# Loading x first, sharing its squares and the weight remainders with GpSimd, and handing PSUM banks over singly, in the first stage of a decoder block

## The chip, the cores and the metric

The kernel runs on one core of a Trainium2 chip. A core has TensorE (matrix products into PSUM; the profile calls its products PE and its weight loads PEld), VectorE (DVE), ScalarE (ACT), GpSimd (POOL) and SyncE (SP), which here only issues transfers (DMA). Each engine works through its own queue of instructions in the order in which they were written into it; between engines, semaphores make an instruction wait. SBUF is the core's working memory of 128 partitions; PSUM holds eight banks of 128 x 512 float32 numbers. The metric is the time of one execution in microseconds (us); lower is better.

## The reference

One block of a decoder with 512 tokens and 2048 channels. What the first stage computes, and what reads it:

```python
c_act = jax.nn.silu(c)
mod = c_act @ w_ada[l] + b_ada[l]                       # 2048 x 12288
sh1, sc1, gt1, sh2, sc2, gt2 = jnp.split(mod[:, None, :], N_MOD, axis=-1)
h = _rmsnorm(x, norm1_g[l]) * (1.0 + sc1) + sh1         # x * rsqrt(mean(x*x) + eps) * g
p = h @ w_in[l]                                         # 2048 x 4384
y_rwkv = _rwkv7_mixer(p[..., :N_RWKV_COLS], ...)
y_pool = _pool_mixer(p[..., N_RWKV_COLS:], ...)
mix = jnp.concatenate([y_rwkv, y_pool], axis=-1) @ w_out[l]
x = x + gt1 * mix
h = _rmsnorm(x, norm2_g[l]) * (1.0 + sc2) + sh2
x = x + gt2 * _conv_ffn(h, w_up[l], conv_w[l], conv_b[l], w_down[l])
...
return _rmsnorm(x, norm_f_g)
```

The RWKV mixer runs eight pairs of heads (0 to 7), each from columns r, k and v of p and from three low-rank tiles that all pairs share; the pooling mixer has four groups of 256 channels.

## The kernel before, in words

Activations lie transposed, channels on partitions, as 16 tiles of 128 x 512. Weights are float32, and a product keeps their precision by a split: `split_weights` (L101) loads a 128 x 512 tile of weights (`wraw`, four buffers), ScalarE casts it to a shorter type (`whi`, L105, three buffers), and VectorE subtracts that from the original (`wlo`, L107, three buffers). Activations are split the same way into `ah` and `al`. `mm3` (L110) then makes three products into one PSUM tile: whi with ah, whi with al, wlo with ah.

The first stage (L168 to L256) goes like this. SP issues the constant tables (`vec`, `cmat` with the identity and the ones, `masks`, `mlev`, `lanei`, `prec`), then c, broadcast to all partitions (`cb`). ScalarE applies silu to cb; a row of it is stored to DRAM (`cact`) for later stages. x arrives in eight transfers of two tiles. For the norm, ScalarE squares each tile of x and VectorE adds it to one sum (`sacc`); four small products with ones (`pst`) sum over the partitions, ScalarE takes the square root, VectorE the reciprocal and spreads it on a diagonal (`rdiag`), one more product (`psb`) broadcasts it, and ScalarE copies it to SBUF (`rs`).

The loop over the 16 tiles k follows, and is called a turn below. Per k, two tiles of w_ada (`wa`, 1 MiB each, four buffers) are each multiplied by cb and summed along the row by one VectorE instruction (`jk`, L202), which gives one column of scale (`part` 1) and of shift (`part` 0). Small VectorE instructions finish them (`gsc`, L204; `mod`, L206). `modulate` (L135) makes `h` on VectorE (L137), `ah` on ScalarE (L138) and `al` on VectorE (L139). Two tiles of weights of the input projection are split, and 24 products go into eight PSUM tiles `pf0` to `pf7`, which fill all eight banks and stay open over the 16 turns.

Behind the loop the eight banks are read out: `shift` (L222) mixes each token with the one before it, on ScalarE and then VectorE, for the three low-rank tiles (`xwa`, `xg1`, `xg2`, which then go through tanh and sigmoid on ScalarE) and for r, k and v of pair 0; the last two banks are copied into `upad` for pooling group 3. The pool of banks `ps0` is then closed, and the pool `psa` (tiles `mm`, `pa`, `pb` and others) takes the same eight banks. In the middle stage, `win_pair` (L591) projects r, k and v of a further pair as three window tiles of 16 x 3 products each, `pool_group` (L258) does a pooling group, `stage_a`, `stage_b` and `stage_c` do a pair of heads, and `ada_rest` (L327) goes on with w_ada in small pieces (`jkr`).

The order on each engine is found when the program is built: a scheduler with its own costs takes instructions by priority, which is the order of the Python code unless `hp()` (L611) raises a block. A tile that reuses memory waits for what used it: by default the first tile in a reused pool waits for everything in the pool that lay there before. With `reuse_waits="tile"`, which the later stages' pools already have, a tile waits only for those earlier tiles whose memory it takes.

Of the kernel before, what the change touches and what calls it, by code (L numbers as in the profile page):

```python
# [53 lines left out]
def block_kernel(ctx, tc, a, out, stop=None, dbg=None):  # L54
# [7 lines left out]
    vec = cp.tile([P, NCOL], F32, tag="vec", name="vec")  # L62
    nc.sync.dma_start(vec, a["vec"][:, :])
    cmat = cp.tile([P, 5, P], F32, tag="cmat", name="cmat")
    nc.sync.dma_start(cmat, a["cmat"][:, :, :])
    ident, bones, bmean, cent, ones = (cmat[:, i, :] for i in range(5))
    masks = cp.tile([P, 4, P], F32, tag="masks", name="masks")
    nc.sync.dma_start(masks, a["mask4"][:, :, :])
    mlev = cp.tile([P, 2, 64], F32, tag="mlev", name="mlev")
    nc.sync.dma_start(mlev, a["mlev"][:, :, :])  # L70
    scanm = cp.tile([P, NC, 129], F32, tag="scanm", name="scanm")
    nc.gpsimd.memset(scanm, 1.0)
    nc.gpsimd.memset(scanm[:, :, 0:1], 0.0)
    lanei = cp.tile([64, 16, 16], F32, tag="lanei", name="lanei")
    nc.sync.dma_start(lanei, a["lanei"][:, :, :])
    prec = cp.tile([P, 16], F32, tag="prec", name="prec")
    nc.sync.dma_start(prec, a["prec"][:, :])

    def col(name, i):
        return vec[:, COLS[name] + i : COLS[name] + i + 1]  # L80
# [17 lines left out]
    b1p = cp.tile([P, KT], F32, tag="b1p", name="b1p")  # L98
    V.tensor_scalar_add(b1p, cols("b_ada", 16, 32), 1.0)

    def split_weights(src):  # L101
        raw = wp.tile([P, WC], F32, tag="wraw", name="wraw", bufs=4)
        nc.sync.dma_start(raw, src)
        hi = wp.tile([P, WC], F32R, tag="whi", name="whi", bufs=3)
        S.copy(hi, raw)  # L105
        lo = wp.tile([P, WC], F32R, tag="wlo", name="wlo", bufs=3)
        V.tensor_tensor(lo, raw, hi[:, :].bitcast(F32), op=ALU.subtract)  # L107
        return hi, lo

    def mm3(ps, wh, wl, xh, xl, start, stop):  # L110
# [54 lines left out]
    p0ctx = ExitStack()  # L165
    p0 = p0ctx.enter_context(tc.tile_pool(name="p0", bufs=1))
    if True:
        cb = p0.tile([P, D], F32, tag="cb", name="cb")  # L168
        nc.sync.dma_start(cb, a["c"][0:1, :].partition_broadcast(P))
        S.activation(cb, cb, AF.Silu)  # L170
        nc.sync.dma_start(cact, cb[0:1, :])
        xs = []
        for i in range(8):
            xt = p0.tile([P, 2, T], F32, tag=f"x{i}", name=f"x{i}")
            nc.sync.dma_start(xt, a["xT"][:, 2 * i : 2 * i + 2, :])
            xs += [xt[:, 0, :], xt[:, 1, :]]
        rstd = p0.tile([P, T], F32, tag="rs0", name="rs0")
        with tc.tile_pool(name="ps00", bufs=1, space=PSUM) as ps00:
            pst = ps00.tile([P, NC], F32, tag="st", name="pst")
            acc = p0.tile([P, T], F32, tag="sacc", name="sacc")  # L180
            for k in range(KT):
                if k == 0:
                    S.activation(acc, xs[k], AF.Square)
                    continue
                sq = p0.tile([P, T], F32, tag="sq", name="sq", bufs=2)
                S.activation(sq, xs[k], AF.Square)
                V.tensor_add(acc, acc, sq)
            rms_stats(pst, acc)
            psb = ps00.tile([P, T], F32, tag="bc", name="psb")
            rms_bcast(psb, rms_rows(p0, pst, NC), NC)  # L190
            S.copy(rstd, psb)
        ps0ctx = ExitStack()
        ps0 = ps0ctx.enter_context(tc.tile_pool(name="ps0", bufs=1, space=PSUM))
        pf = [ps0.tile([P, T], F32, tag=f"pf{i}", name=f"pf{i}") for i in range(8)]
        H = []
        for k in range(KT):
            for part in (1, 0):
                j = part * 16 + k
                wa = p0.tile([P, D], F32, tag="wa", name="wa", bufs=4)
                nc.sync.dma_start(wa, a["ada1"][j, :, :])  # L200
                jk = p0.tile([P, D], BF16, tag="jk", name="jk", bufs=1)
                V.scalar_tensor_tensor(jk, wa, 1.0, cb, op0=ALU.mult, op1=ALU.mult,  # L202
                                       accum_out=mod[:, j : j + 1])
            V.scalar_tensor_tensor(gsc1[:, k : k + 1], mod[:, 16 + k : 17 + k], b1p[:, k : k + 1],  # L204
                                   col("n1", k), op0=ALU.add, op1=ALU.mult)
            V.tensor_add(mod[:, k : k + 1], mod[:, k : k + 1], col("b_ada", k))  # L206
            h = p0.tile([P, T], F32, tag="h", name="h", bufs=2)
            hi, lo = slots(k)
            modulate(hi[:, :], lo[:, :], h, xs[k], rstd, gsc1[:, k : k + 1], mod[:, k : k + 1])
            H.append((hi, lo))  # L210
            for i0 in range(0, 8, WC // P):
                wh, wl = split_weights(a["win0"][k, :, i0 * P : i0 * P + WC])
                for ii in range(WC // P):
                    sl = slice(ii * P, (ii + 1) * P)
                    mm3(pf[i0 + ii], wh[:, sl], wl[:, sl], *H[k], start=k == 0, stop=k == KT - 1)
        p0ctx.close()


        actx = ExitStack()
        ra = actx.enter_context(tc.tile_pool(name="ra", bufs=1))  # L220
        if True:
            def shift(ps, m, dst):  # L222
                S.activation(dst, ps, AF.Copy, scale=drv[:, m : m + 1])
                V.scalar_tensor_tensor(dst[:, 1:T], ps[:, 0 : T - 1], col("mu", m), dst[:, 1:T],
                                       op0=ALU.mult, op1=ALU.add)

            def ring(name):
                return ring16(name)[:, 16:]

            def ring16(name):  # L230
                return ra.tile([P, 16 + T], F32, tag="ring", name=name, bufs=7)

            xwa = ra.tile([P, T], F32, tag="xwa", name="xwa")
            shift(pf[0], 24, xwa)
            S.activation(xwa[0:64, :], xwa[0:64, :], AF.Tanh)
            xg1 = ra.tile([P, T], F32, tag="xg1", name="xg1")
            shift(pf[1], 25, xg1)
            S.activation(xg1, xg1, AF.Sigmoid)
            xg2 = ra.tile([P, T], F32, tag="xg2", name="xg2")
            shift(pf[2], 26, xg2)  # L240
            S.activation(xg2, xg2, AF.Sigmoid)

            def vtile(name):
                return ra.tile([P, T], F32, tag="v", name=name, bufs=2)

            rkv0 = []
            for i, m in ((3, 0), (4, 8), (5, 16)):
                t = vtile("v") if i == 5 else ring("rkv")
                shift(pf[i], m, t)
                rkv0.append(t)  # L250

            upad = [ring16("upad") for i in range(2)]
            for i in range(2):
                V.memset(upad[i][:, 0:16], 0.0)
                S.copy(upad[i][:, 16:], pf[6 + i])  # L255
            ps0ctx.close()  # L256

    def pool_group(gi):  # L258
        win = WINS[gi]
# [30 lines left out]
                last_mix.append(split_act(14 + d, mx))  # L290

    psctx = ExitStack()
    psa = psctx.enter_context(tc.tile_pool(name="psa", bufs=1, space=PSUM))

    def mmtile():
        return psa.tile([P, T], F32, tag="mm", name="mm", bufs=2)
# [314 lines left out]
    def hp():  # L611
        return tc.high_priority(offset=100000)

    pool_group(3)
    with hp():
        q = start_pair(0)
        stage_b(0, q)
    win_pair(1)
    for p in range(NP):
        if p + 1 < NP:  # L620
            if p + 2 < NP:
# [320 lines left out]
```

## Time and profile before

| | |
|---|---|
| median of 3 runs | 2465.12 us (2463.72 to 2469.42) |
| the profiled execution | 2465.06 us, of it 2463.3 us between the first and the last instruction (the span) |
| TensorE products | 2355.7 us busy, 96% of the span |
| VectorE | 1450.8 us, 59% |
| ScalarE | 912.6 us, 37% |
| GpSimd | 2.7 us, 13 instructions, all of them fills |
| DMA | 367.40 MB, 149 GB/s on average |

A row of the order in time has the start, the duration, the engine, the line of the code, the operation, output and inputs by the program's names, shapes, how many were merged into the row, and in brackets how long the engine had been idle and what ended that. In a table of stretches, each engine's busy time stands with its count of instructions in brackets, then TensorE's granted clock, the share of time the 16 DMA engines were busy, and GB/s. A group of instructions has its line, engine and operation, the count, busy time and mean duration in nanoseconds, and the idle time ahead of it.

### The profile page before, as it was taken

What the parts mean: (1) busy time and instruction counts of PE and PEld (TensorE: products, weight loads), DVE (VectorE), ACT (ScalarE), POOL (GpSimd) and SP (SyncE); (2) the same over time, 40 slices, a digit from 0 to 9 for tenths busy, and PEclk for the clock granted to TensorE, in tenths of its full rate; (3) what the DMA queues carried; (4) which work ended last, traced back from release to release, by engine and by line L of the source; (5) the groups of instructions that cost most, each with busy time, mean ns of one, the idle gap of its engine ahead of it and who ended that gap; (6) DMA issues with size and microseconds to landing.
All of it is one profiled execution on the core that took longest, in us unless ns stands there. A gap on an engine that the chain in (4) does not pass through costs nothing.

```text
span 2463.3 us, 37835 instructions
## 1 busy us (share of the span) xinstructions
PE 2355.7 (96%) x14386; PEld 1907.4 (77%) x14386; DVE 1450.8 (59%) x2804; ACT 912.6 (37%) x1476; POOL 2.7 (0%) x13
## 2 busy tenths in 40 slices
PE   4889999999998999999999999999999999999997
PEld 3656666666665999887788888888888888888897
DVE  7987777787774477747634443444344433544467
ACT  3244443444334456533223322333233322323354
POOL 0000000000000000000000000000000000000000
PEclk9999999999999999999999999999999999999999
DMA  9965565566554755537532233223322232322255
GB/s 361 338 222 150 164 184 159 145 182 177 169 167 137 237 183 184 181 103 253 182 97 96 98 95 98 98 96 99 95 98 99 95 99 96 97 98 95 98 156 187
DMA packets 240232, 367.40 MB, mean 149 GB/s; under 512 B 75761, under 2 KB 81073, under 8 KB 235825
## 3 DMA queue, kind: packets, MB, share of 16 engines
q1 hardware_dynamic: 240050, 364.99, 46.8%
q8 instruction: 112, 1.84, 0.3%
q14 instruction: 70, 0.57, 0.1%
HBM read 348.90 MB, written 16.00 MB: 148 GB/s over the span
## 4 chain that ended last, share of the span: by engine, by line
PE 68%; DVE 3%; DMA 2%; ACT 1%; issue 1%; SPq 0%; DVEq 0%; ACTq 0%
PE b L113 21%; PE b L111 21%; PE b L112 21%; DMA slot<-ada 1%; DVE slot L774 1%; PE pa L283 1%; PE mm L111 1%; PE mm L112 1%; PE mm L113 1%; DVE wlo L107 0%; DMA wraw<-wup 0%; DMA war<-ada 0%; DMA mxl<-mixd 0%; DVE x L825 0%; PE pb L522 0%
## 5 line engine op out<-in xcount | busy, mean ns | idle before, releaser
L107 DVE TENSOR_TENSOR wlo<-wraw,whi 128x512 fp32r<-128x512 f32 x844 | 579.8, 689 | 694.6 <-ACT whi L105 681.9
L105 ACT CAST whi<-wraw 128x512 fp32r<-128x512 f32 x844 | 524.1, 622 | 1215.4 <-PE b L112 950.2
L113 PE MATMUL b<-hh,wlo 128*128 128x512 f32 (+1 forms) x1472 | 557.6, 381 | 9.7 <-DVE wlo L107 9.6
L111 PE MATMUL b<-hh,whi 128*128 128x512 f32 (+1 forms) x1472 | 559.2, 380 | 0.0
L112 PE MATMUL b<-hl,whi 128*128 128x512 f32 (+1 forms) x1472 | 558.6, 380 | 0.0
L111 PE MATMUL b<-ah,whi 128*128 128x256 f32 (+1 forms) x1344 | 442.2, 329 | 1.4 <-ACT mxp L286 0.9
L112 PE MATMUL b<-al,whi 128*128 128x256 f32 (+1 forms) x1344 | 441.3, 329 | 0.0
L113 PE MATMUL b<-ah,wlo 128*128 128x256 f32 (+1 forms) x1344 | 441.2, 329 | 0.0
L113 PEld LDWEIGHTS b<-hh,wlo 128*128 128x128 f32 x1472 | 275.6, 188 | 65.8 <-DVE wlo L107 13.3
L111 PEld LDWEIGHTS b<-hh,whi 128*128 128x128 f32 x1472 | 277.2, 188 | 53.1 <-ACT whi L105 0.5
L112 PEld LDWEIGHTS b<-hl,whi 128*128 128x128 f32 x1472 | 277.2, 188 | 52.0
L111 PEld LDWEIGHTS b<-ah,whi 128*128 128x128 f32 x1344 | 255.3, 190 | 26.9 <-ACT ah L131 2.4
L112 PEld LDWEIGHTS b<-al,whi 128*128 128x128 f32 x1344 | 255.5, 190 | 23.5 <-DVE al L132 1.0
L113 PEld LDWEIGHTS b<-ah,wlo 128*128 128x128 f32 x1344 | 255.4, 190 | 22.1 <-DVE wlo L107 0.2
L111 PE MATMUL mm<-ah,whi 128*128 128x512 f32 x432 | 179.1, 415 | 5.0 <-ACT upad L255 5.0
L112 PE MATMUL mm<-al,whi 128*128 128x512 f32 x432 | 178.4, 413 | 0.0
L113 PE MATMUL mm<-ah,wlo 128*128 128x512 f32 x432 | 177.3, 410 | 0.0
L336 DVE SCALAR_TENSOR_TENSOR jkr<-war,cq 128x512 bf16<-128x512 f32 x192 | 131.4, 684 | 20.9 <-DMA war<-ada 19.1
L812 DVE SCALAR_TENSOR_TENSOR x<-b,mod,x 128x512 f32<-128x512 f32 x80 | 59.7, 751 | 110.8 <-PE b L113 110.8
L111 PEld LDWEIGHTS mm<-ah,whi 128*128 128x128 f32 x432 | 82.0, 190 | 32.1 <-issue 10.2
L112 PEld LDWEIGHTS mm<-al,whi 128*128 128x128 f32 x432 | 82.1, 190 | 27.8 <-issue 12.7
L113 PEld LDWEIGHTS mm<-ah,wlo 128*128 128x128 f32 x432 | 82.1, 190 | 22.9 <-issue 6.9
(230 smaller groups left out, 2099.3 us busy)
## 6 DMA issues: line engine op xcount, KB each, us to landing
wraw<-wup SPq DMA_DIRECT2D x368, 256.0 KB, 3.0
wraw<-wdn SPq DMA_DIRECT2D x208, 256.0 KB, 2.7
war<-ada SPq DMA_DIRECT2D x192, 256.0 KB, 3.5
wraw<-win SPq DMA_DIRECT2D x140, 256.0 KB, 4.0
wa<-ada SPq DMA_DIRECT2D x32, 1024.0 KB, 7.1
wraw<-wout SPq DMA_DIRECT2D x128, 256.0 KB, 3.4
slot<-ada SPq DMA_DIRECT2D x64, 256.0 KB, 3.9
sp<-spill SPq DMA_DIRECT2D x21, 256.0 KB, 2.7
```

The lines of the kernel that those rows point to most:

```text
L105: S.copy(hi, raw)
L107: V.tensor_tensor(lo, raw, hi[:, :].bitcast(F32), op=ALU.subtract)
L111: PE.matmul(ps, wh, xh, start=start, stop=False)
L112: PE.matmul(ps, wh, xl, start=False, stop=False)
L113: PE.matmul(ps, wl, xh, start=False, stop=stop)
L283: PE.matmul(ps, pw[:, i, d * P : (d + 1) * P], zs[i], start=i == 0, stop=i == 1)
L336: V.scalar_tensor_tensor(jk, wa, 1.0, cq[0], op0=ALU.mult, op1=ALU.mult, accum_out=modq[:, kq, j : j + 1])
L774: V.scalar_tensor_tensor(jk, wa, 1.0, cbs[kq], op0=ALU.mult, op1=ALU.mult, accum_out=modg[:, kq, j : j + 1])
L812: V.scalar_tensor_tensor(x2[f], ps, mod[:, 80 + f : 81 + f], x2[f], op0=ALU.mult, op1=ALU.add)
```

## The change

- Loads: behind `vec`, the first four x transfers, then c, the other four, then `cmat`. The four other tables are issued in the ninth turn of the loop. The store of `cact` follows silu, which now stands after the eighth square.
- Squares: two sums instead of one. Tiles 1, 4, 7, 10 and 13 are summed by GpSimd into the second sum, the others by VectorE into the first. The squares of tiles 3, 9 and 15 are made on VectorE, the rest on ScalarE. The statistics take eight small products, of each sum in turn. A one-column square root (`warm`) is added; in the built order ScalarE runs it before the first square.
- Remainders: in the first stage `wlo` is subtracted by GpSimd; all other stages keep VectorE, and so does the first window tile's first remainder, which stands before the last `al` in VectorE's queue.
- Handover: all eight banks are shifted or copied out first, and tanh and the two sigmoids follow; in the built order on ScalarE the six shifts come first, then one copy, the tanh with its table load, the second copy, the second table load and the two sigmoids, and then the cast of the second tile of window weights. `psa` gets `reuse_waits="tile"`. `win_pair(1)` is written ahead of `pool_group(3)`, which moves into the raised block.

```diff
-    nc.sync.dma_start(cmat, a["cmat"][:, :, :])
...
-    nc.sync.dma_start(masks, a["mask4"][:, :, :])
...
-    nc.sync.dma_start(mlev, a["mlev"][:, :, :])
...
-    nc.sync.dma_start(lanei, a["lanei"][:, :, :])
...
-    nc.sync.dma_start(prec, a["prec"][:, :])
+
+    def load_tables():
+        nc.sync.dma_start(masks, a["mask4"][:, :, :])
+        nc.sync.dma_start(mlev, a["mlev"][:, :, :])
+        nc.sync.dma_start(lanei, a["lanei"][:, :, :])
+        nc.sync.dma_start(prec, a["prec"][:, :])
...
-    def split_weights(src):
+    def split_weights(src, eng=V):
...
-        V.tensor_tensor(lo, raw, hi[:, :].bitcast(F32), op=ALU.subtract)
+        eng.tensor_tensor(lo, raw, hi[:, :].bitcast(F32), op=ALU.subtract)
...
-        cb = p0.tile([P, D], F32, tag="cb", name="cb")
-        nc.sync.dma_start(cb, a["c"][0:1, :].partition_broadcast(P))
-        S.activation(cb, cb, AF.Silu)
-        nc.sync.dma_start(cact, cb[0:1, :])
         xs = []
-        for i in range(8):
+
+        def load_x(i):
             xt = p0.tile([P, 2, T], F32, tag=f"x{i}", name=f"x{i}")
             nc.sync.dma_start(xt, a["xT"][:, 2 * i : 2 * i + 2, :])
-            xs += [xt[:, 0, :], xt[:, 1, :]]
+            xs.extend([xt[:, 0, :], xt[:, 1, :]])
+
+        cb = p0.tile([P, D], F32, tag="cb", name="cb")
+        for i in range(8):
+            load_x(i)
+            if i == 3:
+                nc.sync.dma_start(cb, a["c"][0:1, :].partition_broadcast(P))
+        nc.sync.dma_start(cmat, a["cmat"][:, :, :])
...
-            acc = p0.tile([P, T], F32, tag="sacc", name="sacc")
+            accs = [p0.tile([P, T], F32, tag=f"sacc{i}", name=f"sacc{i}") for i in range(2)]
+            fresh = [True, True]
             for k in range(KT):
-                if k == 0:
-                    S.activation(acc, xs[k], AF.Square)
-                    continue
-                sq = p0.tile([P, T], F32, tag="sq", name="sq", bufs=2)
-                S.activation(sq, xs[k], AF.Square)
-                V.tensor_add(acc, acc, sq)
-            rms_stats(pst, acc)
+                n = 1 if k % 3 == 1 and k < 14 else 0
+                eng = G if n else V
+                if k == 8:
+                    S.activation(cb, cb, AF.Silu)
+                    nc.sync.dma_start(cact, cb[0:1, :])
+
+                    warm = p0.tile([P, 1], F32, tag="warm", name="warm")
+                    S.activation(warm, eps[:, 0:1], AF.Sqrt)
+                dst = accs[n] if fresh[n] else p0.tile([P, T], F32, tag=f"sq{n}", name="sq", bufs=3 if n == 0 else 2)
+                if k % 6 == 3:
+                    V.tensor_mul(dst, xs[k], xs[k])
+                else:
+                    S.activation(dst, xs[k], AF.Square)
+                if not fresh[n]:
+                    eng.tensor_tensor(accs[n], accs[n], dst, op=ALU.add)
+                fresh[n] = False
+            for i in range(NC):
+                for n in range(2):
+                    PE.matmul(pst[:, i : i + 1], accs[1 - n][:, i * P : (i + 1) * P], ones[:, 0:1], start=n == 0, stop=n == 1)
...
+            if k == 8:
+                load_tables()
             for i0 in range(0, 8, WC // P):
-                wh, wl = split_weights(a["win0"][k, :, i0 * P : i0 * P + WC])
+                wh, wl = split_weights(a["win0"][k, :, i0 * P : i0 * P + WC], G)
...
-            shift(pf[0], 24, xwa)
-            S.activation(xwa[0:64, :], xwa[0:64, :], AF.Tanh)
             xg1 = ra.tile([P, T], F32, tag="xg1", name="xg1")
-            shift(pf[1], 25, xg1)
-            S.activation(xg1, xg1, AF.Sigmoid)
             xg2 = ra.tile([P, T], F32, tag="xg2", name="xg2")
-            shift(pf[2], 26, xg2)
-            S.activation(xg2, xg2, AF.Sigmoid)
+            for i, t in enumerate((xwa, xg1, xg2)):
+                shift(pf[i], 24 + i, t)
...
             ps0ctx.close()
+            S.activation(xwa[0:64, :], xwa[0:64, :], AF.Tanh)
+            S.activation(xg1, xg1, AF.Sigmoid)
+            S.activation(xg2, xg2, AF.Sigmoid)
...
-    psa = psctx.enter_context(tc.tile_pool(name="psa", bufs=1, space=PSUM))
+    psa = psctx.enter_context(tc.tile_pool(name="psa", bufs=1, space=PSUM, reuse_waits="tile"))
...
-    pool_group(3)
+    win_pair(1)
     with hp():
+        pool_group(3)
         q = start_pair(0)
         stage_b(0, q)
-    win_pair(1)
```

## The prediction

> **What bounds the kernel now.** I read the page first, then a table of stretches of the span, then the order in time of one engine at a time.
>
> The page's busy times and its forty slices:
>
> ```profile
> PE 2355.7 (96%) x14386; PEld 1907.4 (77%) x14386; DVE 1450.8 (59%) x2804; ACT 912.6 (37%) x1476; POOL 2.7 (0%) x13
> ...
> PE   4889999999998999999999999999999999999997
> ...
> DVE  7987777787774477747634443444344433544467
> ...
> DMA  9965565566554755537532233223322232322255
> ```
>
> TensorE is busy nearly everywhere but in the first three slices (61.6 us each), where VectorE and the DMA stand at 8 or 9. So any time the first stage gives up should reach the end, as long as what follows stays bound by TensorE. The stretches (PE, weight load, DVE, ACT, POOL busy, granted clock, DMA share, GB/s):
>
> ```profile
> 0.00:10.00 10.00, 0.00 (x0) 0.00 (x0) 0.41 (x4) 1.44 (x2) 0.90 (x9) 1.00 0.76 279
> 10.00:20.00 10.00, 0.00 (x0) 0.00 (x0) 6.23 (x10) 8.42 (x13) 0.00 (x0) 1.00 1.02 389
> 13.00:34.00 21.00, 3.94 (x10) 2.28 (x10) 18.15 (x30) 12.12 (x20) 0.00 (x0) 1.00 1.02 407
> 41.00:149.00 108.00, 85.87 (x340) 66.00 (x339) 104.55 (x142) 26.80 (x43) 0.00 (x0) 0.95 0.87 312
> 149.00:161.00 12.00, 7.04 (x24) 5.32 (x24) 5.32 (x11) 9.45 (x14) 1.76 (x4) 0.82 0.82 222
> 200.00:790.00 590.00, 569.25 (x5376) 393.54 (x5375) 427.96 (x1116) 244.77 (x378) 0.00 (x0) 1.00 0.55 161
> ```
>
> Between 41 and 149 us VectorE works 104.55 of 108 us and TensorE 85.87: the loop over k is bound by VectorE. From 200 to 790 TensorE idles 590 - 569.25 = 20.75 us in all. One turn of the loop, VectorE's row by row, with the one ScalarE row (ah) it waits for:
>
> ```profile
> 126.09 2.28 DVE L202 SCALAR_TENSOR_TENSOR jk<-wa,cb 128x2048 bf16<-128x2048 f32 x1
> ...
> 128.42 0.22 DVE L204 SCALAR_TENSOR_TENSOR gsc<-mod,b1p,vec 128x1 f32<-128x1 f32 x1
> 128.68 0.75 DVE L137 SCALAR_TENSOR_TENSOR h<-x,gsc,rs 128x512 f32<-128x512 f32 x1
> 129.35 2.29 DVE L202 SCALAR_TENSOR_TENSOR jk<-wa,cb 128x2048 bf16<-128x2048 f32 x1
> ...
> 131.56 0.69 DVE L107 TENSOR_TENSOR wlo<-wraw,whi 128x512 fp32r<-128x512 f32 x1
> 132.16 0.15 DVE L206 TENSOR_TENSOR mod<-mod,vec 128x1 f32<-128x1 f32 x1
> 132.23 0.69 DVE L107 TENSOR_TENSOR wlo<-wraw,whi 128x512 fp32r<-128x512 f32 x1
> ...
> 132.35 0.72 ACT L138 ACTIVATE ah<-h,mod 128x512 fp32r<-128x512 f32 x1 [3.42 <-DVE mod L206]
> ...
> 133.11 0.75 DVE L139 SCALAR_TENSOR_TENSOR al<-h,mod,ah 128x512 fp32r<-128x512 f32 x1 [0.19 <-ACT ah L138]
> 133.77 2.28 DVE L202 SCALAR_TENSOR_TENSOR jk<-wa,cb 128x2048 bf16<-128x2048 f32 x1
> ```
>
> A turn is 133.77 - 126.09 = 7.68 us. The second wlo lies under ScalarE's ah, for which VectorE then waits only 0.19 us. That cover matters below.
>
> **The change, part by part.** *1. The weight remainders to GpSimd.* VectorE loses two wlo per k, 2 x 0.69 = 1.38 us busy, but not 1.38 us of the turn. With both gone, mod starts at 131.56 instead of 132.16; ah follows mod by 0.19 (132.35 - 132.16), al follows ah by 0.76 (133.11 - 132.35), and the next jk follows al by 0.66. So only the first wlo's 0.60 us is won; in place of the second one VectorE waits for ah, about 0.8 us. The turn becomes 7.68 - 0.60 = 7.08 us, if nothing else happens. TensorE is no bound then: 85.87 us over the 14 turns in 108 us is some 6.1 us each, of which part is at a reduced clock.
>
> What waits for GpSimd: TensorE's third product, and the queue of transfers, because a wraw buffer comes free only after its subtraction, and the next wa transfer is issued behind it on SP. With three whi and wlo buffers the subtraction for k can run almost a turn ahead, so an operation may take up to about half a turn, 3.5 us, before anyone waits. How long it takes, no row shows: GpSimd only fills memory here.
>
> ```profile
> L316 POOL MEMSET xy<- 128x1024 f32 x1 | 1.0, 956 | 0.0
> ```
>
> That is 0.93 ns for each element written (956/1024). A subtraction reads 2 x 512 and writes 512 elements: 1536 x 0.93 = 1.44 us as an upper end; VectorE's 0.69 us for the same operation as the lower; I take the middle, 1.07 us, since GpSimd's row is the nearer engine but its fill may be bound by its writes. By time alone GpSimd keeps up: 2 x 1.44 = 2.9 of 7.08 us.
>
> The open question is whether a reading GpSimd operation holds up VectorE, whose jk, h and al all read two tiles from SBUF. No row of before has the two together. At one end it costs nothing. At the other both subtractions stop VectorE for their whole length, 2 x 1.44: 7.08 + 2.88 = 9.96 us a turn. I take nothing in the sum and keep the other end as the main rival: each jk is 2.28 or 2.29 us throughout, but with nobody to disturb it, so these rows favour neither.
>
> *2. Start of the stage.* The rows that carry it now, from the squares to the second and the last al:
>
> ```profile
> 9.85 1.91 ACT L170 ACTIVATE cb<-cb 128x2048 f32<-128x2048 f32 x1 [7.83 <-DMA cb<-c]
> ...
> 12.83 11.84 DVE L187 TENSOR_TENSOR sacc<-sacc,sq 128x512 f32<-128x512 f32 x15 [8.78 <-ACT sq L186]
> ...
> 24.72 1.87 PE L145 MATMUL pst<-cmat,sacc 128*128 128x1 f32 x8 [24.72 <-DVE sacc L187]
> ...
> 26.67 1.28 ACT L150 ACT_TABLE_LOAD   x1 [2.93 <-PE pst L145]
> ...
> 28.48 0.87 DVE L154 TENSOR_SCALAR rdiag<-cmat,rstd 128x128 f32<-128x128 f32 x4
> ...
> 29.41 2.07 PE L158 MATMUL psb<-rdiag,cmat 128*128 128x512 f32 x2 [2.82 <-DVE rdiag L154]
> ...
> 31.52 0.58 ACT L191 COPY rs<-psb 128x512 f32<-128x512 f32 x1 [2.26 <-PE psb L158]
> ...
> 40.97 0.75 DVE L139 SCALAR_TENSOR_TENSOR al<-h,mod,ah 128x512 fp32r<-128x512 f32 x1 [0.19 <-ACT ah L138]
> ...
> 148.79 0.74 DVE L139 SCALAR_TENSOR_TENSOR al<-h,mod,ah 128x512 fp32r<-128x512 f32 x1
> ```
>
> Now the squares start only after silu (11.8) and run at VectorE's pace for 11.84 us. After the change they follow the loads, whose sizes the list of issues gives (kilobytes each, us to landing):
>
> ```profile
> wraw<-win SPq DMA_DIRECT2D x140, 256.0 KB, 4.0
> wa<-ada SPq DMA_DIRECT2D x32, 1024.0 KB, 7.1
> ...
> x<-xT SPq DMA_DIRECT2D x8, 512.0 KB, 7.2
> ```
>
> Up to the last x these are vec 0.30 (128 x 595 numbers), x 4.19 and c 1.05 MB (128 x 2048), 5.55 MB; 10 us at 279 GB/s move 2.79 MB, the other 2.76 at 389 GB/s take 7.1 us: last x at 17.1. Behind it VectorE has one square and two sums, priced as the 0.69 us wlo: 19.2. There are now eight products for the statistics instead of four (16 passes instead of 8, 1.87/8 = 0.23 us each), one of the sixteen early: 15 x 0.23 = 3.5 us and 0.1 to begin, to 22.8, 1.6 us more than now. The square root's table load no longer waits for TensorE in the new order, so its 1.28 us vanish from the path: between the products' end (26.59) and rdiag (28.48) lie 1.89 us, then 0.6. rdiag 23.4, psb 24.3 (as 28.48 to 29.41), rs 26.4 (as 29.41 to 31.52), done 27.0; VectorE's first jk (24.3 to 26.6) fits beside it. Then h 27.05, jk 27.7, mod 29.9, al 30.9, and the second al one turn later at 38.0, against 40.97: 3.0 us. The c copy to DRAM waits on SP for silu with all weight loads queued behind it: c's last byte (3.45 MB) is there at 11.7, silu done near 13.6, about when wa is issued now. GpSimd's four sums, 4.3 us, run before 17; the four small tables (0.39 MB, 1 us of DMA) move into the ninth k, where transfers lead by almost two turns; the identity and ones are loaded behind x, ready at about 18, 1 us before use.
>
> *3. The handover.* The last al comes at 38.0 + 14 x 7.08 = 137.1 instead of 148.79 (14 turns of 7.70). Then:
>
> ```profile
> 152.87 0.69 ACT L223 ACTIVATE xg<-pf,drv 128x512 f32<-128x512 f32 x1 [0.17 <-PE pf L113]
> 153.58 1.28 ACT L235 ACT_TABLE_LOAD   x1
> 154.87 0.63 ACT L235 ACTIVATE xwa<-xwa 64x512 f32<-64x512 f32 x1
> 155.44 0.39 PE L113 MATMUL pf<-ah,wlo 128*128 128x512 f32 x1
> ...
> 159.58 1.08 ACT L255 COPY upad<-pf 128x512 f32<-128x512 f32 x2
> 160.52 1.17 ACT L105 CAST whi<-wraw 128x512 fp32r<-128x512 f32 x2
> 160.79 0.77 PE L111 MATMUL mm<-ah,whi 128*128 128x512 f32 x1 [4.96 <-ACT upad L255]
> ```
>
> TensorE idles 4.96 us until the last bank is copied out. After the change it goes straight on with 12 products whose whi is ready (2.7 us). The next whi, however, stands in ScalarE's queue behind six shifts, two copies, two table loads and three functions: from 153.7 three shifts 2.4, copies 1.1, loads 2.6, functions 1.9, cast 0.6, 8.6 in all, so near 162.3 on the clock of before, 6.5 us after TensorE's end at 155.8. The wait shrinks from 4.96 to 6.5 - 2.7 = 3.8 us: 1.1 us won. The lower end is nothing, the upper the whole 4.96.
>
> *4. The rest.* From there to the out-projection the written order differs in small swaps (the pool group is due after the first window tile, the sums of pair 0 follow sooner). It costs nothing by itself; 20.75 us of idle are spread over that stretch, and I allow 4 us either way.
>
> **Sum**, against the profiled run's 2465.06 us (span 2463.3; median 2465.12, so the same): -3.0 for the start, -14 x 0.62 = -8.7 for the turns, -1.1 at the handover: -12.8, 2452.
>
> **Rivals.** *A: the subtractions stop VectorE.* If whichever of GpSimd's subtraction and VectorE's two-input operation starts first holds the other up, each turn is 7.08 + 2 x 1.07, less the 0.8 us in which VectorE waits anyway: about 8.5. The first al slips by one sum to 32.0, the last is at 32.0 + 15 x 8.5 = 159.5, 10.7 late; less 1.1: 2475, slower. At 9.96 us a turn it is 2497. It decides from a turn of 7.86 us up: 0.39 us lost per subtraction. For it: VectorE is 97% busy, so GpSimd can hardly find it idle. Against: GpSimd has half a turn of slack, and if it is always the one that waits, nothing is lost. The Trainium skill, page "SBUF — State Buffer", section "Who interferes with whom", says just this of a VectorE instruction with two SBUF inputs and a GpSimd one that reads SBUF, and calls the sharing an exclusive lock. By that rule the time is 2475; no run here shows it yet. Its "GPSIMD Engine Reference" ("Performance versus the Vector engine") has 4497 ns for 2048 elements, by which I estimate 1.12 us for 512; with it a turn is 8.5 to 8.6.
>
> *B: the transfers bind.* A turn loads 2 x 1 MiB and 2 x 256 KiB, 2.62 MB: 341 GB/s in 7.68 us, 370 in 7.08. The DMA share is already high. If 341 were all, the turn stays 7.68, the last al is at 30.9 + 15 x 7.68 = 146.1: 2461, no change. Against it stand the 407 GB/s of 13 to 34 us.
>
> *C: a part of A.* GpSimd is mostly the one that waits, a turn of 7.65: last al 30.9 + 15 x 7.65 = 145.7, with the handover 4.2 us won: 2461.
>
> **Chances.** My forecast 0.50 (own range 2443 to 2459), A 0.33, B 0.05, C 0.12. Faster by over 0.2% (4.9 us, about what a measurement of this kernel tells from no change): the 0.50 and a good half of B and C, 0.58; within: 0.10; slower: A less its mild end, 0.32. The range runs from 2442 to 2482: above it lies the hard half of A, some 0.12, below it 0.05.
>
> **What would show it.** Right: VectorE's turn near 7.1 us with a wait of some 0.8 us for ah before each al; jk still 2.28 us; GpSimd subtractions of 0.7 to 1.5 us; first al near 31 us; no wait of VectorE or TensorE for GpSimd; TensorE's wait at the handover on whi, not on upad. Wrong: jk, h or al lengthened, or GpSimd spans of two microseconds and more with VectorE idle beside them (A); jk waiting for wa (B); TensorE waiting at the pool group or pair 0 for more than 4 us over now (part 4); or a GpSimd start so slow that its four sums end after 19 us.

## The result and the profile after

The changed kernel takes 2500.86 us (2498.83 to 2505.86) against 2467.27 us (2463.72 to 2470.67) of the kernel before on the same chip: 33.6 us slower, a ratio of 1.0141, with a 95% interval of 1.0124 to 1.0158. The forecast was 2452 us; rival A, in which the subtractions stop VectorE, ended at 2475 us and at its hard end at 2497. The profiled execution took 2501.53 us, its span is 2499.8.

The page of the changed kernel, busy times and forty slices of 62.5 us each:

```profile
PE 2382.2 (95%) x14394; PEld 1923.9 (77%) x14394; DVE 1466.9 (59%) x2770; ACT 911.6 (36%) x1475; POOL 69.3 (3%) x49
...
PE   4779999999999899999999999999999999999997
...
DVE  7988677776675567756734443444344443444467
...
POOL 3330000000000000000000000000000000000000
PEclk9889999899999999999999999999999999999999
```

GpSimd has come in with 69.3 us, all in the first three slices, but VectorE has not become less busy: 1466.9 us instead of 1450.8, although 32 subtractions of 0.69 us have left it. VectorE's rows in order of time show where they went. Columns: start, duration, engine and line, operation, shapes, and in brackets what the engine waited for:

```profile
79.90 1.09 DVE L225 TENSOR_TENSOR mod<-mod,vec 128x1 f32<-128x1 f32 x1
81.78 0.75 DVE L140 SCALAR_TENSOR_TENSOR al<-h,mod,ah 128x512 fp32r<-128x512 f32 x1 [0.79 <-ACT ah L139]
82.45 3.36 DVE L221 SCALAR_TENSOR_TENSOR jk<-wa,cb 128x2048 bf16<-128x2048 f32 x1
...
86.11 0.75 DVE L138 SCALAR_TENSOR_TENSOR h<-x,gsc,rs 128x512 f32<-128x512 f32 x1
86.78 2.28 DVE L221 SCALAR_TENSOR_TENSOR jk<-wa,cb 128x2048 bf16<-128x2048 f32 x1
...
89.11 1.09 DVE L225 TENSOR_TENSOR mod<-mod,vec 128x1 f32<-128x1 f32 x1
90.99 0.75 DVE L140 SCALAR_TENSOR_TENSOR al<-h,mod,ah 128x512 fp32r<-128x512 f32 x1 [0.79 <-ACT ah L139]
```

GpSimd over the same time:

```profile
77.58 3.40 POOL L108 TENSOR_TENSOR wlo<-wraw,whi 128x512 fp32r<-128x512 f32 x1 [3.12 <-ACT whi L106]
82.34 1.33 POOL L108 TENSOR_TENSOR wlo<-wraw,whi 128x512 fp32r<-128x512 f32 x1 [1.36 <-ACT whi L106]
86.95 3.23 POOL L108 TENSOR_TENSOR wlo<-wraw,whi 128x512 fp32r<-128x512 f32 x1 [3.29 <-ACT whi L106]
```

The subtraction that starts at 82.34, ahead of jk (82.45), takes 1.33 us, and jk takes 3.36 instead of 2.28. The one that comes at 86.95, after jk has begun (86.78), shows 3.23 us: it waits until jk ends near 89.0 and then runs, and now it is `mod`, one number per partition, that takes 1.09 us instead of 0.15. So a subtraction that finds VectorE at work waits for it, and then VectorE's next operation waits for the subtraction: whoever is first, VectorE loses about 1 us, 1.08 at jk and 0.94 at `mod`. I counted 1.09 for each, by which a turn is 7.08 + 2 x 1.09 = 9.26 us; the rows give 90.99 - 81.78 = 9.21. The 0.79 us in front of `al`, which were to be the price of the lost cover, are there as forecast, and GpSimd makes no use of them.

The start of the stage in the changed kernel, VectorE, then GpSimd's last two sums and two rows of ScalarE:

```profile
15.53 4.76 DVE L203 TENSOR_TENSOR sacc<-sacc,sq 128x512 f32<-128x512 f32 x4 [0.55 <-ACT sq L201]
20.22 0.68 DVE L199 TENSOR_TENSOR sq<-x 128x512 f32<-128x512 f32 x1
20.82 1.41 DVE L203 TENSOR_TENSOR sacc<-sacc,sq 128x512 f32<-128x512 f32 x2
25.76 0.18 DVE L152 RECIPROCAL rstd<-rstd 128x4 f32<-128x4 f32 x1 [3.53 <-ACT rstd L151]
25.97 0.87 DVE L155 TENSOR_SCALAR rdiag<-cmat,rstd 128x128 f32<-128x128 f32 x4
...
29.63 0.75 DVE L138 SCALAR_TENSOR_TENSOR h<-x,gsc,rs 128x512 f32<-128x512 f32 x1 [0.32 <-ACT rs L210]
30.30 3.35 DVE L221 SCALAR_TENSOR_TENSOR jk<-wa,cb 128x2048 bf16<-128x2048 f32 x1
...
33.69 1.09 DVE L225 TENSOR_TENSOR mod<-mod,vec 128x1 f32<-128x1 f32 x1
35.58 0.75 DVE L140 SCALAR_TENSOR_TENSOR al<-h,mod,ah 128x512 fp32r<-128x512 f32 x1 [0.79 <-ACT ah L139]
...
16.41 3.34 POOL L203 TENSOR_TENSOR sacc<-sacc,sq 128x512 f32<-128x512 f32 x2 [2.79 <-ACT sq L201]
...
11.78 1.28 ACT L192 ACT_TABLE_LOAD   x1
13.07 1.91 ACT L192 ACTIVATE cb<-cb 128x2048 f32<-128x2048 f32 x1
```

The last sum ends at 22.2 and not at the 19.2 of the forecast, for two reasons. Four sums beside GpSimd's take 4.76 us, where six take 4.60 with GpSimd idle (the last run below, in which the last sum ends at 20.7). And silu, with a table load ahead of it, ends at 15.0 and not near 13.6, so that ScalarE's remaining squares start that much later. The first `al` stands at 35.58 (before 35.62, forecast 30.9), the second at 44.81 (before 40.97) and the last at 173.89, 25.1 us later than before.

The handover, TensorE:

```profile
180.86 0.39 PE L114 MATMUL pf<-ah,wlo 128*128 128x512 f32 x1
181.09 0.39 PE L112 MATMUL mm<-ah,whi 128*128 128x512 f32 x1
...
183.58 0.39 PE L114 MATMUL mm<-ah,wlo 128*128 128x512 f32 x1
186.63 0.50 PE L112 MATMUL mm<-ah,whi 128*128 128x512 f32 x1 [2.66 <-ACT whi L106]
```

`mm` follows `pf` at once, runs 12 products, and waits 2.66 us for whi: the step as forecast (3.8 us), and 25.1 us late have become 20.3 (181.1 against 160.8).

From the first mm to the last, TensorE does the same 5,512 products in both kernels, in another order. As stretches (length, then busy time with counts of TensorE, weight load, VectorE, ScalarE and GpSimd, then the granted clock, DMA share and GB/s), the kernel before:

```profile
160.80:785.90 625.10, 606.16 (x5512) 418.47 (x5512) 458.70 (x1186) 260.49 (x399) 0.00 (x0) 0.99 0.56 163
```

and the changed kernel, with 13 us out of this stretch:

```profile
181.10:826.30 645.20, 621.43 (x5513) 427.33 (x5511) 459.47 (x1189) 265.87 (x407) 0.00 (x0) 0.97 0.55 160
...
462.00:475.00 13.00, 13.00 (x57) 8.22 (x56) 6.68 (x14) 1.80 (x4) 0.00 (x0) 0.50 0.57 166
```

Here another 20.1 us go: 4.8 more of idle time (23.8 against 18.9, the wait for whi among it), and 15.3 us of longer products, of which 13 us at a clock of 0.50 explain about 6.5 by my estimate, half of the stretch. So the last mm ends 40.4 us late; some 4 us of it come back before the end, and 36.5 remain in the profiled spans.

### The profile page after: what moved, and what is told of

It reads as the page before. It is cut to its first block, busy times and chain, and to the rows that moved or that the text cites. A ratio compares the mean times of both kernels' runs of the same rounds, so it can differ in the third digit from the quotient of the medians.

```text
span 2499.8 us, 37848 instructions
## 1 busy us (share of the span) xinstructions
PE 2382.2 (95%) x14394; PEld 1923.9 (77%) x14394; DVE 1466.9 (59%) x2770; ACT 911.6 (36%) x1475; POOL 69.3 (3%) x49
## 4 chain that ended last, share of the span: by engine, by line
PE 81%; DMA 5%; DVE 4%; issue 1%; ACT 1%; SPq 0%; DVEq 0%; ACTq 0%
PE b L112 21%; PE b L114 21%; PE b L113 20%; PE mm L112 3%; PE mm L114 3%; PE mm L113 3%; DMA war<-ada 1%; PE pb L542 1%; PE pb L540 1%; DVE wlo L108 1%; PE pb L533 1%; PE pa L303 1%; DMA wraw<-wup 1%; DMA wraw<-wout 1%; PE pa L422 1%
## 5 line engine op out<-in xcount | busy, mean ns | idle before, releaser
L108 DVE TENSOR_TENSOR wlo<-wraw,whi 128x512 fp32r<-128x512 f32 x812 | 557.8, 689 | 694.1 <-ACT whi L106 680.3
```

What stands on the lines that cost most here:

```text
L108: eng.tensor_tensor(lo, raw, hi[:, :].bitcast(F32), op=ALU.subtract)
```

## The experiments

The first theory is the lock seen in these rows, 1.09 us per subtraction. Its rival is a GpSimd that is merely slow. For the 20 us of the middle there are three candidates: the new order of the middle, the clock, and TensorE running ahead at the handover. Each comparison is with the kernel before on the same chip (2468.3, 2466.66 and 2466.74 us for the three groups of four runs).

**The remainders alone.**

```
-                wh, wl = split_weights(a["win0"][k, :, i0 * P : i0 * P + WC])
+                wh, wl = split_weights(a["win0"][k, :, i0 * P : i0 * P + WC], G)
```

> The kernel before with one edit: the two weight remainders of each k in the first stage go to GpSimd. Theory, a lock: whichever of GpSimd's subtraction and a two-input VectorE operation starts first holds the other up, 1.09 us for each subtraction, so a turn is 7.08 + 2 x 1.09 = 9.26 us; the last al comes some 22 us later than in the kernel before (148.8 to about 171), TensorE's waits after it stay as they were, and the time is about 2490 us. Rival, GpSimd is merely slow and TensorE waits for it: jk stays 2.28 us and VectorE idles at the head of its operations instead. Second question: the order of the middle stages is that of the kernel before here; if the changed kernel lost its further 17 us there by its order, the delay of 22 us stays the same to the end of this run; if the loss came from the later start or from a lower clock that any order has, this run ends near 2507 us.

Measured: 2491.55 us, ratio 1.0084 (1.006 to 1.0109); 23.2 us more than before. VectorE's turn in this run:

```profile
99.63 1.09 DVE L206 TENSOR_TENSOR mod<-mod,vec 128x1 f32<-128x1 f32 x1
101.52 0.75 DVE L139 SCALAR_TENSOR_TENSOR al<-h,mod,ah 128x512 fp32r<-128x512 f32 x1 [0.79 <-ACT ah L138]
102.19 3.38 DVE L202 SCALAR_TENSOR_TENSOR jk<-wa,cb 128x2048 bf16<-128x2048 f32 x1
...
105.61 1.12 DVE L204 SCALAR_TENSOR_TENSOR gsc<-mod,b1p,vec 128x1 f32<-128x1 f32 x1
```

The same 1.09 us on jk, `mod` and `gsc`; its turns are 9.2 us, the last `al` is at 175.38. And the middle, in which every one of the 5,512 products stands where it stands in the kernel before:

```profile
187.40:813.50 626.10, 607.90 (x5512) 420.33 (x5512) 459.87 (x1186) 260.48 (x400) 0.00 (x0) 0.99 0.56 163
```

626.1 us against 625.1: what the first stage loses is handed through, and nothing of note is added. A late start alone does not cost the middle anything.

**GpSimd writes but doesn't read.**

```
+        if eng is G:
+            G.memset(lo[:, :].bitcast(F32), 0.0)
+        else:
             V.tensor_tensor(lo, raw, hi[:, :].bitcast(F32), op=ALU.subtract)
```

> As the run with only the remainders on GpSimd, but GpSimd fills the low tile with zeros and reads nothing (the low part of the weights is left out of the computation). Theory, the lock belongs to GpSimd operations that read SBUF: jk stays 2.28 us, the turn is the 7.08 us of the forecast, the last al is some 9 us earlier than before, about 2458 us. Rival, any GpSimd access to SBUF stops VectorE: turns above 8 us and about 2475 to 2490 us.

Measured: 2457.74 us, ratio 0.9948 (0.9927 to 0.9968). Every jk is 2.28 or 2.29 us beside fills of 0.52, and the turn is 98.27 - 91.07 = 7.20:

```profile
91.07 0.75 DVE L142 SCALAR_TENSOR_TENSOR al<-h,mod,ah 128x512 fp32r<-128x512 f32 x1 [0.79 <-ACT ah L141]
91.74 2.29 DVE L205 SCALAR_TENSOR_TENSOR jk<-wa,cb 128x2048 bf16<-128x2048 f32 x1
...
98.27 0.75 DVE L142 SCALAR_TENSOR_TENSOR al<-h,mod,ah 128x512 fp32r<-128x512 f32 x1 [0.79 <-ACT ah L141]
```

This is near the forecast's turn (7.08), and shows what the removal would have been worth in the first stage if it were free: the last `al` comes at 141.46, 7.3 us earlier than before. The medians differ by 10.6 us, but this run also has the higher clock, 0.992 or 0.993 against 0.986 to 0.991 in the kernel before on the same chip; so no more than the 7.3 is shown.

**VectorE reads one tile, not two.** The dot product becomes a plain sum:

```
-                V.scalar_tensor_tensor(jk, wa, 1.0, cb, op0=ALU.mult, op1=ALU.mult,
-                                       accum_out=mod[:, j : j + 1])
+                V.reduce_sum(mod[:, j : j + 1], wa, axis=mybir.AxisListType.X)
```

> As the run with only the remainders on GpSimd, but jk becomes a plain sum over wa, with one input from SBUF instead of two (the factor c is left out of the computation). Theory, the lock is between a GpSimd operation and a VectorE operation with two inputs from SBUF: the sum is not held up, the turn is 7.1 to 7.4 us, some 9 us faster than before, 2460 us. Rival, any VectorE operation that reads SBUF is held up: the sum grows by 1.09 us for each subtraction, and the time is 2490 us as with two inputs.

Measured: 2459.97 us, ratio 0.9974 (0.9962 to 0.9986). GpSimd subtracts twice a turn as in the changed kernel, in 1.26 to 1.56 us (some 0.2 us more where it starts while `h`, with its two inputs, still runs), and VectorE is not held:

```profile
104.31 2.28 DVE L202 TENSOR_REDUCE mod<-wa 128x1 f32<-128x2048 f32 x1
106.63 0.16 DVE L205 TENSOR_TENSOR mod<-mod,vec 128x1 f32<-128x1 f32 x1
107.57 0.75 DVE L139 SCALAR_TENSOR_TENSOR al<-h,mod,ah 128x512 fp32r<-128x512 f32 x1 [0.79 <-ACT ah L138]
```

So it takes two: a GpSimd operation that reads, and a VectorE operation with two inputs.

**GpSimd reads one tile.**

```
+            G.tensor_copy(lo, raw)
```

> As the run with only the remainders on GpSimd, but GpSimd copies the raw weights into the low tile instead of subtracting, so it reads one tile and not two (the low part of the weights is left out, the products with it take the full weights instead). Theory, any GpSimd operation that reads SBUF holds VectorE's two-input operations for as long as it reads: some 0.5 to 1.1 us for each, a turn of 8.1 to 9.3 us, 2475 to 2490 us. Rival, only a GpSimd operation with two inputs does so: jk stays 2.28 us, the turn is 7.2 us and the time that of the fill, 2458 us.

Measured: 2467.5 us, ratio 1.0005 (0.9992 to 1.0018). Fifteen turns take 7.48 to 8.55 us, 7.83 in the mean. VectorE is held, less and not always:

```profile
84.27 1.10 DVE L140 SCALAR_TENSOR_TENSOR h<-x,gsc,rs 128x512 f32<-128x512 f32 x1
85.30 2.28 DVE L205 SCALAR_TENSOR_TENSOR jk<-wa,cb 128x2048 bf16<-128x2048 f32 x1
...
96.05 1.17 DVE L142 SCALAR_TENSOR_TENSOR al<-h,mod,ah 128x512 fp32r<-128x512 f32 x1 [0.79 <-ACT ah L141]
```

`h` loses 0.35 us and `al` 0.42, so a copy (0.61 us on GpSimd) costs about a third of a subtraction, less than I expected; over the run it is 0.3 us for each, (7.83 - 7.20) / 2. One input on GpSimd is enough for the effect.

**One remainder of two.**

```
+                wh, wl = split_weights(a["win0"][k, :, i0 * P : i0 * P + WC], V if i0 else G)
```

> The kernel before with only the first of the two remainders of each k on GpSimd, the second stays on VectorE beneath ah. Theory, each subtraction costs VectorE 1.09 us wherever it falls, and the one that is taken away gives 0.60 us: a turn of 7.68 - 0.60 + 1.09 = 8.17 us, 14 x 0.49 = 7 us later, 2475 us. Rival, with half the subtractions GpSimd finds its place in VectorE's gaps: a turn of 7.1 to 7.3 us and 2460 us.

Measured: 2481.24 us, ratio 1.0063 (1.0049 to 1.0077); 14.5 us more, twice what I expected. The lock is as expected (jk 3.37), but the turn is 95.75 - 86.98 = 8.77, not 8.17. The planner put VectorE's remaining wlo ahead of `mod`, and so out of the cover of `ah`:

```profile
85.43 0.69 DVE L107 TENSOR_TENSOR wlo<-wraw,whi 128x512 fp32r<-128x512 f32 x1
86.04 0.15 DVE L206 TENSOR_TENSOR mod<-mod,vec 128x1 f32<-128x1 f32 x1
86.98 0.75 DVE L139 SCALAR_TENSOR_TENSOR al<-h,mod,ah 128x512 fp32r<-128x512 f32 x1 [0.79 <-ACT ah L138]
```

That gives 7.68 + 1.09 = 8.77: nothing gained by the move, the whole lock paid.

**The start alone** (x first, three engines, sums on GpSimd, table loads moved; the edit is the first half of the change's diff).

> The kernel before with the start of the stage alone: x loaded first, squares on ScalarE, VectorE and every third sum on GpSimd, table loads moved. Theory: the gain of 3 us is eaten by GpSimd's four sums, so the first al stands near 35.6 us as before; what the changed kernel had later at its second al (44.8 against 41.0) was the subtractions, so here the second al is near 41 to 42.7 and the time within 2 us of before, 2467 us. Rival, the start as such is late for another reason than GpSimd (loads of x and c, the products for the statistics), by more than 2 us: 2470 us and more, and then a start without GpSimd has the same lateness.

Measured: 2464.92 us, ratio 0.9981 (0.997 to 0.9992), 3.4 us less than before and so a little outside the 2 us that I expected. The first `al` is at 33.68, the second at 41.36 (before 40.97), the last at 149.93 (before 148.79), mm starts at 160.90 (before 160.79), and the profiled span is 0.8 us shorter than before. The interval leaves out no change, but the first stage has gained nothing, so I can't say what the 3.4 us of the medians are. The expectation of a first `al` as late as before was wrong by 2 us. What that `al` hides: in the kernel before VectorE had already done the next jk when it came to it, and here it hasn't.

**The handover alone** (tanh and sigmoid deferred, banks one by one, window pair ahead of the pool group; the second half of the diff).

> The kernel before with the handover part alone: tanh and sigmoid behind the six shifts, PSUM banks handed over one by one, the second window pair ahead of the pool group. Theory, the order of the middle costs what was lost there: the first product of the next weights starts some 3 us earlier than before, and the last pool group then ends 10 to 17 us later than the handover says; 2474 to 2481 us. Rival, the middle lost its time for another reason (the moved start of the loads, the clock): 2464 us, 3 us faster than before.

Measured: 2474.51 us, ratio 1.0023 (1.0009 to 1.0038), 6.2 us more. TensorE's mm starts at 154.32 instead of 160.79 and yet the run ends later:

```profile
154.30:794.50 640.20, 616.24 (x5513) 422.04 (x5511) 458.47 (x1191) 265.89 (x407) 0.00 (x0) 0.99 0.56 162
```

640.2 us for the middle, 15.1 more than before, at the same mean clock. 4.8 of them are its waits for whi and wlo in the first 10 us, which in the kernel before lie ahead of mm; the other 10.1 are longer products. The last mm ends 8.6 us later than before.

**One wait less, same order.** Of the handover only this, by which no instruction changes its place:

```
-    psa = psctx.enter_context(tc.tile_pool(name="psa", bufs=1, space=PSUM))
+    psa = psctx.enter_context(tc.tile_pool(name="psa", bufs=1, space=PSUM, reuse_waits="tile"))
```

> The kernel before with one wait less: the PSUM pool of the middle takes over the banks of the first stage one by one, all instructions in the order of before; TensorE's first product behind the last pf no longer waits for the copies into upad. Theory, handing over the banks is worth what TensorE can do ahead of the next whi, 12 products of 0.23 us, and costs nothing later as the order stays: mm starts at 156 instead of 160.8, waits some 3 us for whi behind its first products, and the time is 2 to 3 us shorter, 2465.5 us. Rival, the later loss of the changed kernel comes from TensorE running ahead here, not from the order: 2468 us or more.

Measured: 2466.48 us, ratio 0.9998 (0.9988 to 1.0009): no change, and neither theory was tested by it, for mm, the next product behind a pf that starts at 154.34, still waits:

```profile
159.46 0.80 PE L111 MATMUL mm<-ah,whi 128*128 128x512 f32 x1 [4.73 <-DVE rkv L224]
```

With ScalarE's copy gone from its list, the next one on it takes its place: VectorE's shifts, for which it waits only 0.23 us less (4.73 against 4.96), with tanh and sigmoids still standing between them.

**The deferral alone, and the swap alone.** Deferral:

```
-            shift(pf[0], 24, xwa)
-            S.activation(xwa[0:64, :], xwa[0:64, :], AF.Tanh)
...
+            for i, t in enumerate((xwa, xg1, xg2)):
+                shift(pf[i], 24 + i, t)
...
+            S.activation(xwa[0:64, :], xwa[0:64, :], AF.Tanh)
```

> The kernel before with tanh and the two sigmoids written behind the six shifts and the two copies, nothing else; the planner then lays out the whole middle anew (some 1,000 of 17,000 products at another place). Theory, the new order is what costs: mm starts 3 to 5 us earlier than in before and the last mm ends 5 to 10 us later, 2473 to 2478 us. Rival, the order is neutral and the deferral gains its 3 us: 2465 us.

Measured: 2476.22 us, ratio 1.0047 (1.0029 to 1.0064). mm starts at 157.98, 2.8 us earlier than before, and the last mm ends 12.9 us later:

```profile
158.00:798.80 640.80, 617.17 (x5512) 421.19 (x5512) 455.47 (x1184) 262.13 (x401) 0.00 (x0) 0.99 0.55 161
```

Swap:

```
-    pool_group(3)
+    win_pair(1)
     with hp():
+        pool_group(3)
...
-    win_pair(1)
```

> The kernel before with the second window pair written ahead of the pool group and of pair 0, nothing else: again the planner lays out the middle anew (some 900 of 17,000 products at another place), with the handover of before. Theory, a new order costs 10 to 15 us wherever it comes from: 2478 to 2483 us. Rival, it is the deferral's order alone that costs: 2468 us.

Measured: 2475.86 us, ratio 1.004 (1.0024 to 1.0055), with the handover of before; the last mm ends 7.0 us later:

```profile
159.40:792.90 633.50, 609.68 (x5512) 417.27 (x5512) 456.49 (x1186) 260.12 (x399) 0.00 (x0) 0.99 0.55 162
```

Three edits, three new orders of the middle, 8 to 16 us longer in each. In the runs that keep the order of before, product by product, the same stretch takes 626.1 us (remainders alone), 630.2 (one wait less) and 628.1 (the last run below), so a single profile is good to some 5 us here; but the medians part the same way, since each of the three new orders is slower by its interval and the old order with one wait less is not. That these new orders cost 6 to 10 us of the medians is thus shown. Where they cost it is shown less well. The idle time is 5 us more (23.6 to 24.0 against 18.9), but with the handover alone that is the wait for whi and wlo. The products are 10.1 us longer with the handover and 11.0 with the deferral; with the swap 3.5 us, which is no more than one run in the old order shows (3.6, one wait less). What makes the products longer, these runs do not settle.

**The remainders undone in the changed kernel.**

```
-                wh, wl = split_weights(a["win0"][k, :, i0 * P : i0 * P + WC], G)
+                wh, wl = split_weights(a["win0"][k, :, i0 * P : i0 * P + WC])
```

> The changed kernel with one part undone: the weight remainders are back on VectorE; the start, the handover and the new order of the middle stay. Theory, the parts add up: what the remainders alone cost (23 us in their own run) goes, what the handover's order costs (6 to 9 us) and what the start gains (0 to 3 us) stay, so the turn is 7.7 us, the last al near 150 us and the time about 2473 us. Rival, the remainders and the order make each other worse, by the lower clock of the changed kernel's middle: then this run comes out near 2467 us and the remainders' share of the changed kernel's loss is over 30 us.

Measured: 2473.77 us, ratio 1.0037 (1.0024 to 1.0051), 7.0 us more than before, as the first theory had it. Its middle takes 636.0 us, 9.2 less than in the changed kernel. But it is not the changed kernel's middle: TensorE's order between the first and the last mm is here that of the handover alone, but for one pair of neighbours, while in the changed kernel another product stands at 2,550 of the 5,512 places. The planner laid the middle out anew when the subtractions moved, so this edit undoes the remainders and an order together. The 33.6 - 7.0 = 26.6 us between the two kernels are what both are worth; the remainders alone took 23.2.

Adding the three parts run by themselves gives 23.2 + 6.2 - 3.4 = 26.0 of 33.6 us. The other 7.6 us can be the changed kernel's own order, which no other run has, or its lower clock: 0.982 or 0.983 in each of its executions, 0.985 or 0.986 with the remainders alone, 0.986 to 0.991 with them undone. Which of the two it is, and why its clock is the lowest, stays open.

**A start without GpSimd, with a jk ahead of the statistics.** x first as in the change; squares on ScalarE and three on VectorE, one sum on VectorE; the middle in the order of before.

```
+        wa0 = load_wa(0, 1)
+        nc.sync.dma_start(cmat, a["cmat"][:, :, :])
+        wa1 = load_wa(0, 0)
...
+            dot(0, 1, wa0)
             for i in range(NC):
...
+                    PE.matmul(pst[:, i : i + 1], accs[n][:, i * P : (i + 1) * P], ones[:, 0:1], start=True, stop=True)
```

> The kernel before with another start: x first, squares on ScalarE and three on VectorE, one sum on VectorE alone and nothing on GpSimd, and the first dot product of the modulation written and loaded ahead of the statistics, so that VectorE does it while TensorE, ScalarE and VectorE's own rdiag are waited for. The middle has the order of before. Theory, the start is VectorE's work without a hole, as the loop is: what the start alone left idle before rdiag (3.5 us) is filled, the first al comes near 30 us, the second near 38 us instead of 41, and the time is 3 to 6 us below before, 2462 to 2465 us. Rival, the first stage is bound by its transfers from here on: the last al stays near 149 us and the time at 2467 us.

Measured: 2461.21 us, ratio 0.998 (0.9965 to 0.9995). This one is faster than both kernels, by 5.5 us of medians against before; the interval only just leaves out no change. The profiled execution, 2464.82 us, is one of the slower ones of this run, and its span is merely 0.3 us shorter. Its VectorE:

```profile
19.30 1.41 DVE L216 TENSOR_TENSOR sacc<-sacc,sq 128x512 f32<-128x512 f32 x2
20.62 2.29 DVE L189 SCALAR_TENSOR_TENSOR jk<-wa,cb 128x2048 bf16<-128x2048 f32 x1
...
23.30 0.87 DVE L155 TENSOR_SCALAR rdiag<-cmat,rstd 128x128 f32<-128x128 f32 x4
...
28.57 0.75 DVE L140 SCALAR_TENSOR_TENSOR al<-h,mod,ah 128x512 fp32r<-128x512 f32 x1 [0.79 <-ACT ah L139]
```

jk fills the 3.5 us in which VectorE stood idle in the changed kernel. The second `al` is at 37.45 against 40.97, the last at 145.97 against 148.79, and mm starts 3.9 us earlier, at 156.87.

## Why the prediction was wrong, step by step

*1, the remainders.* The step that failed is "I take nothing in the sum" for the question whether a reading GpSimd operation holds up VectorE. It does: about 1 us for each subtraction (1.08 at jk, 0.94 at `mod`), where only one of VectorE's own two took 0.60 of the turn and the other nothing. The other half of the step was right to some 0.1 us: without the lock the turn is 7.2 us (forecast 7.08; the run with the fill), with the 0.79 us wait for `ah`. The price of 1.07 us that I had taken for a subtraction, halfway between bounds, was meant as its time on GpSimd, which is 1.33 us; that it came near the hold was luck. Rival A had the mechanism, but two things in it were off. I let the hold overlap the 0.8 us in which VectorE waits anyway (8.5 us a turn); in the turns shown GpSimd sat idle there for 1.36 us, waiting for whi, and so a turn is 9.2 us. And "Against: GpSimd has half a turn of slack, and if it is always the one that waits, nothing is lost" was the wrong picture: a GpSimd operation that has waited for jk goes first when jk ends, and holds `mod` or `gsc`.

The Trainium skill's page "SBUF — State Buffer", sections "SBUF: two separate sides" and "Who interferes with whom", says that a VectorE operation with two SBUF inputs and a GpSimd operation that reads SBUF exclude each other for a whole instruction, and that the first to start wins. The runs agree on who holds whom: no hold beside a fill, none beside a one-input sum, about 1 us with two inputs against a subtraction. In length the hold was less than the instruction's 1.33 us in the trace.

I had given rival A 0.33. The rows of before spoke neither for it nor against it, so the nothing in the sum stood there without a reason.

*2, the start.* Forecast 3.0 us won at the second `al`; measured 3.8 us lost, 0.4 of which remain when the remainders stay on VectorE. Two steps failed. "GpSimd's four sums, 4.3 us, run before 17": they ran until 19.8, in 1.27 to 1.7 us each, and VectorE's own sums took longer beside them, as under the same lock. And "silu done near 13.6" left out the table load of 1.28 us ahead of it: silu ended at 15.0. So the last sum ended at 22.2 and not at 19.2; without GpSimd's sums, in the last run, it ended at 20.7. The square root's table load did go from the path (sqrt at 25.46, 0.04 us behind the products). With the remainders on VectorE the first `al` is at 33.71, 2.8 us behind the forecast of 30.9; what the changed kernel lost beyond that by its second `al` is the hold.

*3, the handover.* The mechanism was right (12 products, then whi); the wait was 2.66 us, not 3.8, so that some 2.3 us were won there instead of 1.1.

*4, the rest.* "It costs nothing by itself" failed, and so did "4 us either way": the three runs with a new order and the old first stage ended 6.2 to 9.6 us later, the 6.2 with the handover's gain in it. The 20.75 us of idle time were the wrong bound: in two of the three orders two thirds of the loss is in longer products (10.1 of 15.1 us and 11.0 of 15.7). What the changed kernel's own order costs was not run by itself.

Rivals B and C are out. For B, no jk waited for wa, and with the write-only fill the same transfers were done in turns of 7.2 us; for C, the turn is 9.2 us and not 7.65.

## What to carry to other kernels

Where VectorE is the bound, as in this loop, count a GpSimd helper that reads SBUF as VectorE's own work, at what it holds, unless VectorE's operations have one SBUF input or GpSimd only writes. Before work is taken off an engine, look at what it does in its pauses: the second remainder was free already. And when an edit lets a planner lay out a tuned stage anew, the new order is a cost to be bounded by itself: build the edit so that the order stays, or run the new order alone, and see from the trace which order a run has: undoing one part can lay out the stage once more.

## What the runs showed that I had not expected

A held VectorE operation need not be large: `mod` and `gsc`, 128 x 1, take 1.09 to 1.12 us instead of 0.15 and 0.22 when they come up behind a waiting GpSimd. The hold is shorter than GpSimd's busy span (0.94 to 1.08 of 1.33 us for a subtraction, 0.35 to 0.42 of 0.61 for a copy in the rows shown). And TensorE's granted clock fell to 0.50 for 13 us in the middle of the changed kernel (462 to 475 us), where the kernel before shows 1.00 in every 20 us from 240 to 780; over the executions of one kernel the time goes with the mean clock: with the remainders undone, 2469.5 us at 0.991 and 2485.4 at 0.986.
